# One transformer-like layer on one core: modulation sums by TensorE, smaller first pieces of tile 0, and a second copy in the Fourier stage

## The chip, the core and the metric

The kernel runs on one core of a Trainium2 chip. The core has five engines with an instruction queue each: TensorE (PE, matrix products, with its weight loads shown apart as PEld), VectorE (DVE), ScalarE (ACT), GpSimd (POOL) and SyncE (SP, which here only issues transfers). Each engine works through its instructions in the order in which they stand in its program and waits at an instruction until its semaphores allow it. Transfers are issued by SP, ACT and POOL into DMA queues and moved by 16 DMA engines. Products go into eight PSUM banks of 128 x 512 floats; everything else lies in SBUF, with 128 partitions.

The metric is the device time of one execution in microseconds. An L with a number is a line of the kernel before, unless the changed kernel is meant and said.

## The reference, cut to what matters

One layer is computed for two groups of tokens that share parameters: 256 context tokens and 2,048 latent tokens, each with 1,024 channels, which makes 18 tiles of 128 rows. All of it is fp32.

```python
def adaln(cvec, w_mod, b_mod):                 # modulation: two vectors (c and c_ctx)
    m = jax.nn.silu(cvec) @ w_mod + b_mod      # 1024 -> 6 x 1024
    return jnp.split(m[:, None, :], 6, axis=-1)

sh1, sc1, g1, sh2, sc2, g2 = adaln(...)
h = rms_norm(x, norm1_g) * (1 + sc1) + sh1
q, k, v, f = split(h @ w_in)                   # 4 x 512 columns
attn = softmax(q0 k0) v - lam * softmax(q1 k1) v          # 4 heads, latent keys + 512 cached keys
spec = fft2(f, axes=(positions, 128 channels), norm='ortho').real   # 4 channel groups
four = spec @ w_four                           # per channel group
x = x + g1 * (concat(rms_norm(attn), four) @ w_out)
x = x + g2 * relu(rms_norm(x)*(1+sc2)+sh2 @ w1)**2 @ w2
```

Only the first two parts of `m` (shift `sh1`, scale `sc1`) are needed before the first tile's projection. The 2-D transform is done as real matrix products: over the positions with cosine and sine matrices, then over the channels.

## The kernel before, in words

**Order of the work.** The kernel is one long function, `body`, that runs through its stages in turn: modulation and the first tile; projection of the 18 tiles; the Fourier stage; attention of the four heads; output projection and MLP. In most places the instructions stand on each engine in the order in which the code issues them (`manual_schedule`); tiles in the middle of the projection and later stages are ordered by a scheduler. Each matrix product that needs fp32 accuracy is made of three with a high and a low part of each operand (L94, L95, L96 in `mm3`): high x high, high activation x low weight, low activation x high weight.

**Modulation (L464 to L538).** Eight blocks `wm` of 128 rows of `w_mod` are loaded, 2,048 columns each (the 1,024 of the shift and the 1,024 of the scale). Columns 0 to 1,279 are multiplied by PE (`pr`, L484, two rows for two conditioning vectors). Columns 1,280 to 2,047 are summed up by VectorE: `acc[s]` for each of the two vectors `s`, 128 x 768, to which each block adds its rows times a number per partition (L486 to L490). In between stand the normalization of the first tile's rows and PE's transposes of them (L495, into the two banks `pt0`). At the end the sums must become columns. For the PE part, ScalarE copies `pr` to `mr` and PE transposes it in pieces of 128 into `pm` (L535, ten small transposes). For the VectorE part, what is left is the sum over the 128 partitions: VectorE transposes blocks of 32 and adds within them (`TRANSPOSE_TENSOR_REDUCE`, L528, once for each `s`) and PE adds the four blocks with a matrix of shifted ones, `quad0`, which GpSimd has made at the start (L474, `quads`): four products into `pq` (L537). VectorE then adds the bias into `modc` and makes `scale1 = (1 + scale) * gain` (`mk_scale`).

**Tile 0.** The weights `w_in` come in sixteen half blocks of 1,024 columns (`w_half`, L504; k is the block of 128 rows, h the half), of which six buffers exist. ScalarE rounds them to the high part (`w_high`, L513), VectorE subtracts for the low part (`w_rest`, L516), and each second `w_rest` asks for the half block six further on, by a DMA on SP's queue. Tile 0's transposed rows are scaled and shifted out of PSUM into `h0` (`h_first`, in two pieces of four column blocks) and split into a high and a low part, `hh` and `hl` (L554, L555). The projection `pj` of tile 0 follows block by block, so that its products start as soon as the first half of `hh` is there, and each block's four column groups `g` wait for that block's weights.

**Fourier (L643 to L985).** Its pools are opened in the order `f_t`, `f_y`, `f_l` on the left side of SBUF. A pool lies behind the one opened ahead of it, and pools with `reuse_waits="tile"` take over memory of closed pools: a new tile waits for whatever still uses the bytes that it takes.

```python
ft = c2.enter_context(tc.tile_pool(name="f_t", bufs=2, reuse_waits="tile"))
yp = c2.enter_context(tc.tile_pool(name="f_y", bufs=1, reuse_waits="tile"))
```

For each channel group g of four, `f_y` holds `ys{g}`, 128 x 2,048 floats, into which all results of that group are put. The work runs over levels named `p` (context tokens), `o`, `e`, `f` and `l` by size. In a level PE first makes two products over the positions (`pab`, evacuated by ScalarE into `abe`, `abf`, `abl` and so on, L792 and L810), and then `yT` (L749) makes two over the channels, `py` (L753) and `pz` (L755), that rotate through three PSUM banks. ScalarE copies `py` to an SBUF buffer `yu` (L759). VectorE subtracts and adds the pair into two halves of `ys` (L767, L768), reading `yu` from SBUF and `pz` from PSUM. `yu` has two buffers in `f_t` for widths up to 256, and four in `f_l` for the widest level, where `pz` is copied also (`yv`) and the additions are put off. When the last level has filled `ys{g}`, GpSimd's queue issues its store of 1 MiB into the scratch `four` in HBM (L829); the stores of g = 0, 1, 2, 3 follow one another.

**Attention.** Its pools follow when those of the Fourier stage are closed (L992 to L1000): `a_t`, then `a_p` with five buffers `P0` of 10,240 bytes per partition, on the same side of SBUF, and PSUM as 5 + 2 + 1 banks. For a block of 128 queries PE makes scores `Ss` of 512 keys at a time (`fill`, L1080), VectorE takes their maximum over the row (`rowmax`, L1085, and `comb`, L1088), ScalarE takes the exponential from the PSUM bank into `P0` or `P1` (`exp`, L1104), which empties the bank, GpSimd scales and combines the two halves (L1119, L1120), and PE transposes the result (L1135) for the product with the values. The first two groups use all eight banks for scores (`Group.bank`, L1059), so PE may be eight banks ahead of ScalarE.

## Time and profile before

| | |
|---|---|
| median of 3 runs | 2862.53 us (2861.9 to 2864.64) |
| the profiled execution | 2863.18 us, its span 2861.4 us |
| mean granted TensorE clock | 0.999 |
| modulation and tile 0 | from the start to about 60 us |
| Fourier stage | ends at about 520 us |
| attention's first exponential | at 522.70 us |

The profile is of one execution; its times count from the span's start. How rows read: a line of engines says busy time, share of the span and number of instructions. A row of the waits names an engine, the instruction that waited, the engine and instruction that released it, the total in us, how often, and the longest. A row of the order in time has the start and the duration in us, the engine, line, operation, out<-in, their shapes, how many, and in square brackets how long the engine had been idle ahead of it and what released it. A row of the windows has the stretch, its length, and then the busy time (with the count of instructions) of PE, PEld, DVE, ACT and POOL, the granted clock, the share of the DMA engines and GB/s. A row of the groups has busy time, the mean ns of one, and the idle time just ahead with its releaser.

### The profile page before, as it was taken

The numbers are of one execution on the slowest core, as the hardware profiler recorded it, in microseconds if no ns is written. First come the engines' busy times: TensorE is split into PE (matmuls) and PEld (weight loads), VectorE is DVE, ScalarE is ACT, GpSimd is POOL, SyncE is SP. The second block draws the span as 40 slices with busy tenths as digits, with TensorE's granted clock in tenths as the row PEclk, the third lists the DMA queues.
The fourth block names the chain that finished last, engine by engine and source line by source line (L and its number), as shares of the span: only waits on it lengthen the run. The fifth ranks groups of instructions, "written<-read, shape, count | busy, mean of one in ns | idle before, by whom it ended". The sixth has DMA issues, their size and how long they took to land.

```text
span 2861.4 us, 43224 instructions
## 1 busy us (share of the span) xinstructions
PE 2831.7 (99%) x15109; PEld 2455.9 (86%) x15109; DVE 2018.0 (71%) x3393; ACT 1548.2 (54%) x3505; POOL 1073.3 (38%) x890
## 2 busy tenths in 40 slices
PE   8999999999999999999999999999999999999999
PEld 5888888688888888888889999999998888888887
DVE  7767886898988989864477777778775354345554
ACT  4333323798989989853356565556555332333221
POOL 1211223798999989942223333333332000000000
PEclk9999999999999999999999999999999999999999
DMA  7776777421211212036767676667747464445663
GB/s 284 219 207 198 230 213 237 172 106 38 73 71 53 106 38 99 23 124 201 242 221 232 223 246 228 221 219 238 234 167 255 147 202 135 138 144 185 206 206 111
DMA packets 392780, 492.94 MB, mean 172 GB/s; under 512 B 26467, under 2 KB 306384, under 8 KB 389490
## 3 DMA queue, kind: packets, MB, share of 16 engines
q1 hardware_dynamic: 387136, 479.73, 50.9%
q0 software_dynamic: 1872, 7.28, 0.8%
q10 hardware_dynamic: 3554, 3.17, 0.4%
q8 instruction: 119, 1.95, 0.3%
q14 instruction: 99, 0.81, 0.1%
HBM read 312.58 MB, written 179.59 MB: 172 GB/s over the span
## 4 chain that ended last, share of the span: by engine, by line
PE 54%; DVE 1%; DMA 0%; ACT 0%; issue 0%; SPq 0%; POOL 0%; DVEq 0%; POOLq 0%
PE ps L94 8%; PE ps L95 8%; PE ps L96 8%; PE pB L1749 2%; PE pB L1747 2%; PE pB L1748 2%; PE pA L1748 2%; PE pC L1748 2%; PE pA L1749 2%; PE pC L1747 2%; PE pA L1747 2%; PE pC L1749 2%; PE po L94 2%; PE po L96 2%; PE po L95 2%; PE pD L1749 1%
## 5 line engine op out<-in xcount | busy, mean ns | idle before, releaser
L1085 DVE TENSOR_REDUCE mxs<-Ss 128x1 f32<-128x512 f32 x636 | 405.4, 686 | 65.5 <-PE Ss L1080 55.1
L1420 DVE TENSOR_TENSOR sl<-sr,sh 128x768 fp32r<-128x768 f32 x168 | 161.8, 964 | 331.5 <-ACT sh L1419 331.1
L1120 POOL TENSOR_TENSOR P0s<-P0s,P1s 128x1024 f32<-128x1024 f32 (+2 forms) x128 | 378.6, 2958 | 10.7
L1419 ACT CAST sh<-sr 128x768 fp32r<-128x768 f32 x168 | 140.6, 838 | 418.3 <-PE ps L95 418.3
L1789 POOL TENSOR_TENSOR gs<-g,g 128x384 f32<-128x384 f32 x48 | 69.7, 1452 | 468.5 <-ACT g L1759 418.9
L1104 ACT ACTIVATE P1s<-Ss,mxs 128x512 f32<-128x512 f32 x318 | 215.4, 694 | 36.3 <-DVE mxs L1088 35.3
L94 PE MATMUL pj<-wh,hh 128*128 128x512 f32 x576 | 228.8, 397 | 2.0 <-DVE hh L555 2.0
L94 PE MATMUL ps<-thT,sh 128*128 128x512 f32 x585 | 227.6, 389 | 0.0
L95 PE MATMUL ps<-tlT,sh 128*128 128x512 f32 x585 | 227.6, 389 | 0.0
L96 PE MATMUL ps<-thT,sl 128*128 128x512 f32 x585 | 227.6, 389 | 0.0
L95 PE MATMUL pj<-wl,hh 128*128 128x512 f32 x576 | 227.1, 394 | 0.5 <-DVE wl L516 0.5
L96 PE MATMUL pj<-wh,hl 128*128 128x512 f32 x576 | 225.6, 392 | 0.0
L1104 ACT ACTIVATE P0s<-Ss,mxs 128x512 f32<-128x512 f32 x318 | 214.3, 691 | 5.6 <-DVE mxs L1088 5.0
L1135 PE MATMUL pts<-ident,P0s 128*128 128x128 f32 x1280 | 191.7, 273 | 4.5 <-DVE als L1147 1.8
L1080 PE MATMUL Ss<-KS0s,Qs 128*128 128x512 f32 x636 | 190.1, 419 | 0.4 <-ACT P1s L1104 0.4
L1080 PE MATMUL Ss<-KS1s,Qs 128*128 128x512 f32 x636 | 188.7, 420 | 1.5 <-ACT P0s L1104 1.4
L1758 ACT ACTIVATE g<-uz 128x384 f32<-128x384 f32 x144 | 75.7, 526 | 200.2 <-DVE uz L1781 174.1
L1135 PEld LDWEIGHTS pts<-ident,P0s 128*128 128x128 f32 x1280 | 151.3, 140 | 35.9 <-issue 4.8
L1119 POOL TENSOR_SCALAR P1s<-P1s,tots 128x1024 f32<-128x1024 f32 (+2 forms) x128 | 171.9, 1343 | 5.8
L1147 DVE TENSOR_TENSOR als<-pts,ahs 128x512 fp32r<-128x512 f32 x256 | 165.9, 681 | 6.9 <-ACT ahs L1142 6.7
L94 PE MATMUL ps<-ophT,sh 128*128 128x512 f32 x423 | 164.7, 389 | 1.1 <-DVE uz L1781 1.1
L96 PE MATMUL ps<-ophT,sl 128*128 128x512 f32 x423 | 164.6, 389 | 0.0
(536 smaller groups left out, 8073.9 us busy)
## 6 DMA issues: line engine op xcount, KB each, us to landing
sr<-sd SPq DMA_DIRECT2D x84, 768.0 KB, 4.5
a<-in_w SPq DMA_DIRECT2D x184, 256.0 KB, 4.2
sd<-gs SPq DMA_DIRECT2D x192, 192.0 KB, 1.9
sd<-g SPq DMA_DIRECT2D x144, 192.0 KB, 2.1
wm<-in_w_mod SPq DMA_DIRECT2D x32, 512.0 KB, 5.2
Qs<-qd SPq DMA_DIRECT2D x32, 512.0 KB, 4.0
b<-in_w SPq DMA_DIRECT2D x64, 256.0 KB, 5.8
b<-tsum SPq DMA_DIRECT2D x64, 256.0 KB, 4.7
```

The source lines that it names most:

```text
L94: nc.tensor.matmul(ps, lh, rh, start=first, stop=False)
L95: nc.tensor.matmul(ps, lh, rl, start=False, stop=False)
L96: nc.tensor.matmul(ps, ll, rh, start=False, stop=last)
L1080: nc.tensor.matmul(S[:, :w], self.Q[:, x, m, j * P:j * P + P], self.hd.KS[m][:, b * 512:b * 512 + w], start=(x == 0), stop=(x == 1))
L1085: nc.vector.tensor_reduce(self.mx[j][:, m, b:b + 1], self.S[j, m, b], axis=AX.X, op=ALU.max)
L1104: nc.scalar.activation(dst, S, AF.Exp, bias=self.mx[j][:, m, 6:7], accum_out=self.sm[j][:, m, b:b + 1])
L1119: nc.gpsimd.tensor_scalar(p, p, tot[:, 3:4], 0.0, op0=ALU.mult, op1=ALU.add)
L1120: nc.gpsimd.tensor_add(d, d, p)
L1135: nc.tensor.transpose(pt[:, c:c + P], self.p0[j][:, (kb + t) * P:(kb + t + 1) * P], ident)
L1747: nc.tensor.matmul(ps, wh[:, c], hh[:, k, :], start=first and k == 0, stop=False, skip_group_check=True)
L1748: nc.tensor.matmul(ps, wh[:, c], hl[:, k, :], start=False, stop=False, skip_group_check=True)
L1749: nc.tensor.matmul(ps, wl[:, c], hh[:, k, :], start=False, stop=k == 3, skip_group_check=True)
```

## The change

It has three parts.

*Modulation.* `quad0`, VectorE's two transposing reductions and the four products with them are gone. PE makes the sums over the partitions by twelve products, six for each `s`: 128 columns of `acc[s]` as the stationary matrix and the column `ones` as the moving one, straight into `pq` (L540 of the changed kernel). `s` runs as (1, 0) here and in the sums over the blocks. The transposes of the tile's column blocks 6 and 7 move from ahead of the last `wm` block to the small transposes.

*Tile 0.* `h_first(b)`, which did four column blocks, becomes `h_pieces(ks)`, called with (0, 1), (2, 3) and (4 to 7); the scale is made for the first two blocks alone and then for the others (`scale_part`). The weights' steps `w_high` and `w_rest` of column groups 0 and 1 are issued ahead of the scaling, with them the request for half block 6; `w_high` of groups 2 and 3 stands between the pieces.

*Fourier.* `yu` has four buffers in `f_t` too. For the widths 256 and 128 ScalarE copies `pz` also, to the upper half of `yu`, and VectorE's subtraction and addition read SBUF alone. For 129 columns (levels `p` and `l`) `pz` is read from PSUM as before.

```diff
                     setup_cond(p1, pps, rw)
-                    z = quads(t2, "quad0")
+                    for n in range(2):
+                        t2(f"place{n}")
...
-                        for s in range(2):
+                        for s in (1, 0):
                             wk, sc = wm[k][:, 1280:2048], cols[:, 8 * s + k:8 * s + k + 1]
...
-                        if 3 <= k < 7:
+                        if 3 <= k < 6:
...
-                    sums = t2("sums0")[:, 0:48].rearrange("p (s c) -> p s c", s=2)
-                    for s in range(2):
-                        nc.vector.tensor_reduce(sums[:, s, :], acc[s].rearrange("p (c i) -> p c i", i=32), axis=AX.X, op=ALU.add,
-                                                apply_transpose=True)
+                    w_high(0, 0)
+                    w_rest(0, 0)
                     for gi in range(3):
...
+                        if gi == 2:
+                            for x in (6, 7):
+                                nc.tensor.transpose(at0(x), X[0][:, x * P:(x + 1) * P], ident)
+                            X.pop(0)
                         for j in range(w // P):
                             nc.tensor.transpose(pm[:, gi * 4 + j, :], r[0:2, j * P:(j + 1) * P], ident[0:2, 0:2])
-                    for q in range(4):
-                        nc.tensor.matmul(pq, z[:, 96 - 32 * q:224 - 32 * q], sums[:, :, q::4], start=(q == 0), stop=(q == 3))
-                    for g in range(4):
-                        w_high(0, g)
-                    w_rest(0, 0)
...
-                    mk_scale(scale1, 8, 80)
+                    for s in (1, 0):
+                        for j in range(6):
+                            nc.tensor.matmul(pq[:, s, j:j + 1], acc[s][:, j * P:j * P + P], ones, start=True, stop=True)
+                    w_high(0, 1)
+                    w_rest(0, 1)
...
-                    def h_first(b):
-                        for k in range(4 * b, 4 * b + 4):
...
+                    def h_pieces(ks):
+                        for k in ks:
...
+                    nc.vector.tensor_add(modc[:, 0:10, :], pm, cols[:, 32:42].unsqueeze(2).to_broadcast([P, 10, 2]))
+                    scale_part(slice(0, 2))
+                    h_pieces((0, 1))
+                    nc.vector.tensor_add(modc[:, 10:16, :], pq.rearrange("p s j -> p j s"), cols[:, 42:48].unsqueeze(2).to_broadcast([P, 6, 2]))
+                    scale_part(slice(2, KD))
+                    for g in (2, 3):
+                        w_high(0, g)
+                    h_pieces((2, 3))
...
-                            if k or g:
+                            if k or g > 1:
                                 w_rest(k, g)
...
-                            h_first(1)
+                            h_pieces((4, 5, 6, 7))
...
-                u, v = (yl if late else ft).tile([P, 512], F32, tag="yu", name="yu", bufs=4 if late else 2)[:, :w], pz[:, :w]
+                yu = (yl if late else ft).tile([P, 512], F32, tag="yu", name="yu", bufs=4)
+                u, v = yu[:, :w], pz[:, :w]
                 nc.scalar.copy(u, py[:, :w])
...
+                elif w != HW:
+                    v = yu[:, 256:256 + w]
+                    nc.scalar.copy(v, pz[:, :w])
```

Three places in the order of the instructions show it. A row has the line, the operation, out<-in with the tiles' numbers, the shape, and the semaphores that it waits for; `x3` stands for three more of the kind.

PE at the end of the modulation, before: small transposes of `mr` into `pm10`, the four products with `quad0`, and the first three projections of tile 0.

```order
L535 MATMUL pm10_402<-ident_175,mr1_413 128x2 [waits Activation_49]
L535 MATMUL pm10_402<-ident_175,mr1_413 128x2 x3
L535 MATMUL pm10_402<-ident_175,mr2_419 128x2 [waits Activation_49]
L535 MATMUL pm10_402<-ident_175,mr2_419 128x2
L537 MATMUL pm6_403<-sums0_404,quad0_249 128x12 [waits DVE_49,Pool_49]
L537 MATMUL pm6_403<-sums0_404,quad0_249 128x12 x3
L94 MATMUL pj0_0_456<-wh0_0_337,hh0_436 128x512 [waits DVE_49]
L95 MATMUL pj0_0_456<-wl0_0_345,hh0_436 128x512
L96 MATMUL pj0_0_456<-wh0_0_337,hl0_437 128x512 [waits DVE_49]
```

The same place in the changed kernel; `macc_l` and `macc_h` are the two `acc[s]`.

```order
L537 MATMUL pm10_397<-ident_175,mr1_407 128x2 [waits Activation_49]
L537 MATMUL pm10_397<-ident_175,mr1_407 128x2 x3
L534 MATMUL pta0_1_255<-ident_175,x0_226 128x128 x2
L537 MATMUL pm10_397<-ident_175,mr2_413 128x2 [waits Activation_49]
L537 MATMUL pm10_397<-ident_175,mr2_413 128x2
L540 MATMUL pm6_398<-ones_182,macc_l_257 128x1 [waits DVE_49]
L540 MATMUL pm6_398<-ones_182,macc_l_257 128x1 x5
L540 MATMUL pm6_398<-ones_182,macc_h_256 128x1 [waits DVE_49]
L540 MATMUL pm6_398<-ones_182,macc_h_256 128x1 x5
L94 MATMUL pj0_0_465<-wh0_0_332,hh0_435 128x512 [waits DVE_49]
L95 MATMUL pj0_0_465<-wl0_0_340,hh0_435 128x512
```

The transposes of `x0` now stand among the small ones, and twelve products with `ones`, which wait for VectorE's last sums, take the place of the four that waited for VectorE's reductions.

ScalarE in the Fourier stage, before, from the last `yu` of level `e` to level `f`.

```order
L759 COPY yu_5073<-py_5069 128x256 [waits DVE_49,PE_49]
L792 COPY abf0_0_5083<-pabf0_0_5081 128x128 [waits PE_49]
L792 COPY abf0_1_5087<-pabf0_1_5085 128x128 [waits PE_49,Activation_49]
L759 COPY yu_5093<-py_5089 128x256 [waits PE_49]
L792 COPY abf1_0_5099<-pabf1_0_5097 128x128 [waits PE_49]
L792 COPY abf1_1_5103<-pabf1_1_5101 128x128 [waits PE_49,Activation_49]
L759 COPY yu_5109<-py_5105 128x128 [waits PE_49]
```

The same place in the changed kernel.

```order
L773 COPY yu_5081<-py_5077 128x256 [waits DVE_49,PE_49]
L779 COPY yu_5081<-pz_5079 128x256 [waits PE_49]
L809 COPY abf0_0_5092<-pabf0_0_5090 128x128 [waits PE_49]
L809 COPY abf0_1_5096<-pabf0_1_5094 128x128 [waits PE_49,Activation_49]
L773 COPY yu_5102<-py_5098 128x256 [waits DVE_49,PE_49]
L779 COPY yu_5102<-pz_5100 128x256 [waits PE_49]
L809 COPY abf1_0_5109<-pabf1_0_5107 128x128 [waits PE_49]
L809 COPY abf1_1_5113<-pabf1_1_5111 128x128 [waits PE_49,Activation_49]
L773 COPY yu_5119<-py_5115 128x128 [waits DVE_49,PE_49]
```

Each copy of `py` into `yu` has a copy of `pz` into the same buffer behind it.

ScalarE at the passage from the Fourier stage to the attention, before: the last copies of the Fourier stage and the first exponential.

```order
L810 COPY abl3_0_5204<-pabl3_0_5201 128x130 [waits PE_49]
L810 COPY abl3_1_5209<-pabl3_1_5206 128x130 [waits PE_49,Activation_49]
L759 COPY yu_5215<-py_5211 128x129 [waits PE_49]
L759 COPY yu_5224<-py_5220 128x129 [waits PE_49]
L1104 ACTIVATE P0s0_0_0_5294,sms0_0_0_5271<-Ss0_0_0_0_0_5273,mxs0_0_0_5270 128x512 [waits DVE_49,Pool_49]
```

The same place in the changed kernel.

```order
L827 COPY abl3_0_5218<-pabl3_0_5215 128x130 [waits PE_49]
L827 COPY abl3_1_5223<-pabl3_1_5220 128x130 [waits PE_49,Activation_49]
L773 COPY yu_5229<-py_5225 128x129 [waits PE_49]
L773 COPY yu_5238<-py_5234 128x129 [waits PE_49]
L1121 ACTIVATE P0s0_0_0_5308,sms0_0_0_5285<-Ss0_0_0_0_0_5287,mxs0_0_0_5284 128x512 [waits DMASW0_49,DVE_49,Pool_49]
```

The first exponential, which waited for VectorE and for GpSimd, now waits for a DMA of GpSimd's queue as well (`DMASW0`). By the counts behind these names in the two programs it is the queue's last transfer in the Fourier stage, the store of `four` from `ys3`.

20 lines of the change are left out of this document (11 added, 9 removed).

## The prediction

> **What bounds the kernel now.** I read the page first, then TensorE's list of waits for the two stretches that the change touches, then the order in time at each wait found there.
>
> ```profile
> span 2861.4 us, 43224 instructions
> PE 2831.7 (99%) x15109; PEld 2455.9 (86%) x15109; DVE 2018.0 (71%) x3393; ACT 1548.2 (54%) x3505; POOL 1073.3 (38%) x890
> PE pj L94 <- DVE hh L555: 2.0, 1, 2.0
> PE ptckT L358 <- DMA ck<-in_cache_k: 1.2, 2, 0.9
> PE pj L95 <- DVE wl L516: 0.5, 1, 0.5
> PE pz L755 <- DVE ys L768: 1.4, 1, 1.4
> 560.00:600.00 40.00, 40.00 (x264) 34.21 (x264) 35.34 (x72) 36.85 (x103) 37.91 (x28) 1.00 0.25 96
> ```
>
> TensorE (PE) is busy for 99% of the span, and the three lines after it are all that it waited for by name from 30 to 492 us: 3.7 us. So an edit can win only what stands in such lines, and whatever newly stops PE is lost whole. The Fourier stage adds one wait of 1.4 us (fourth line of waits). In the attention (last row: 40 us in which PE is busy for 40.00) there is no idle time that could give a loss back. All terms below are against this execution, 2863.18 us with a span of 2861.4; it lies 0.65 above the median, 2862.53. What a measurement here can tell from no change is about 0.2%, 5.7 us.
>
> **Tile 0 and the modulation.**
>
> ```profile
> 28.53 0.93 DVE L528 TRANSPOSE_TENSOR_REDUCE sums<-macc_l 128x24 f32<-128x768 f32 x1
> 28.59 0.85 PE L535 MATMUL pm<-ident,mr 2*128 2x2 f32 x10
> 29.61 1.03 PE L537 MATMUL pm<-sums,quad 128*128 128x12 f32 x8 [0.17 <-DVE sums L528]
> 32.62 0.79 PE L94 MATMUL pj<-wh,hh 128*128 128x512 f32 x1 [1.98 <-DVE hh L555]
> 31.00:32.00 1.00, 0.00 (x0) 0.00 (x0) 0.93 (x4) 0.88 (x4) 0.00 (x0) 0.50 1.00 410
> 37.00:38.00 1.00, 1.00 (x4) 0.81 (x3) 1.00 (x3) 1.00 (x3) 0.00 (x0) 0.65 0.95 332
> 47.26 2.39 ACT L513 CAST wh<-win 128x512 fp32r<-128x512 f32 x4 [0.65 <-DMA win<-in_w_in]
> 53.67 2.50 DVE L516 TENSOR_TENSOR wl<-win,wh 128x512 fp32r<-128x512 f32 x4 [0.28 <-ACT wh L513]
> 55.25 0.50 PE L94 MATMUL pj<-wh,hh 128*128 128x512 f32 x1
> 56.23 0.50 PE L95 MATMUL pj<-wl,hh 128*128 128x512 f32 x1 [0.47 <-DVE wl L516]
> ```
>
> Removed: VectorE's (DVE's) two reductions (one shown, 0.93; the pair takes 1.9) and four fp32 products that run as 8 passes in 1.03 us, 0.129 each. Added: twelve products with the column of ones, 24 passes; at 0.129 that is 3.1 us. They stand behind the ten small transposes, which end at 29.44, so PE is free at about 32.5. Tile 0's first pieces don't hold it up: VectorE needs the sum into `modc`, two steps of the scale, one scaled piece, a copy and a subtraction of half the size, some 1.8 us from about 29.9. So the first projection starts at 32.5 against 32.62 now: nothing won, unless the passes run at half clock (the row 31 to 32 has a granted clock of 0.50), which would make it up to 33.4.
>
> That start doesn't set the end of the stage. The last rows do: PE lost 0.75 us between its products at 55.25 and 56.23 (0.98 from start to start, against 0.23 in steady state), because the last weight's low part came from a chain that begins with a load (ScalarE waited 0.65 us for it at 47.26) and then runs without a gap over ScalarE (ACT) and VectorE. The change requests one weight load some 4 us sooner, since the low part of column group 1 no longer stands behind the scaling, and every later step of VectorE about 0.6 us later. With the early load out of the queue's way I take the 0.75 us as won. Bounds: 2.3 us won if the products keep the clock up (the 11 steps from 32.62 to 37.48 take 4.86 us and would take 2.5 at full clock), 1.0 lost if VectorE's 0.6 and a late start both come through. I take 0.75, nearest to the stall in the rows. The quad matrix on GpSimd (four small steps in the first 2.6 us) costs nothing now and wins nothing.
>
> **Fourier.**
>
> ```profile
> 509.56 0.39 PE L753 MATMUL py<-abf,cw 128*128 128x128 f32 x2
> 511.39 0.49 PE L755 MATMUL pz<-abf,cw 128*128 128x128 f32 x2 [1.44 <-DVE ys L768]
> 510.71 0.62 DVE L768 TENSOR_TENSOR ys<-yu,pz 128x256 f32<-128x256 f32 x1
> 503.09 0.84 DVE L777 TENSOR_TENSOR ys<-yu 128x256 f32<-128x256 f32 x1
> L792 ACT COPY abe<-pabe 128x256 f32<-128x256 f32 x6 | 2.2, 372 | 4.2 <-PE pabe L800 4.2
> ```
>
> PE's one stall here is 1.44 us: the product `pz` needs a bank that VectorE empties at 511.33, behind other work. With ScalarE copying `pz` the bank is free after one copy, so the stall goes: 1.44 won. Added: four copies of 256 and four of 128 columns, priced like its `abe` and `abf` copies, 0.37 and 0.27, 2.6 us in all; they lie in its idle time (4.2 us before six copies in the last row). If that cover were gone, PE would wait for each `ab` copy. VectorE's 16 operations now read both operands from SBUF; between 0.62 (now) and 0.84 (a 128x256 operation on SBUF beside busy GpSimd) the eight wide ones would cost it at most 1.8 us, and that makes the stores below later, not PE.
>
> **Where the new buffers lie.** `yu` has four buffers where it had two: 4,096 bytes per partition more in pool `f_t`, and `f_y` and `f_l` are laid out behind it. By the addresses in the two built programs `ys3` moves from bytes 75,776-83,968 to 79,872-88,064, and the attention's first `P0` block begins at 84,608 in both. Before, the last store (`four` from `ys3`) and the first exponential shared nothing; now the block overlaps the store's source by 3,456 bytes, and the exponential waits for it (third order excerpt above).
>
> ```profile
> 516.49 0.55 POOL L829 DMA_DIRECT2D four<-ys  x1 [5.55 <-DVE ys L768]
> 520.05 0.53 POOL L829 DMA_DIRECT2D four<-ys  x1 [0.35 <-issue]
> DMA to landing us min/median/max: 9.0/11.5/14.7
> q0 software_dynamic: 159, 1.13, 89.2%
> DMA packets 319, 1.28 MB, mean 427 GB/s; under 512 B 42, under 2 KB 172, under 8 KB 181
> 522.70 0.69 ACT L1104 ACTIVATE P0s<-Ss,mxs 128x512 f32<-128x512 f32 x1 [4.04 <-DVE mxs L1088]
> 529.35 0.74 ACT L1104 ACTIVATE P0s<-Ss,mxs 128x512 f32<-128x512 f32 x1
> 523.53 1.40 PE L1080 MATMUL Ss<-KS1s,Qs 128*128 128x512 f32 x4 [1.12 <-ACT P0s L1104]
> ```
>
> The four stores of 1 MiB each queue behind one another, so I give the last, issued at 520.05, the longest of the landing times, 14.7: it lands at 534.75. The first exponential starts at 522.70 now. In the changed kernel the stage is 0.75 + 1.44 us earlier, so the store lands at 534.75 - 2.19 = 532.56, and the exponential starts there: 9.86 us later than now. Queued behind it on ScalarE are all other exponentials, which run without a gap (ten in 6.65 us by the rows at 522.70 and 529.35). PE fills eight banks of scores and then waits (at 523.53 it waited for the first exponential already); VectorE's maxima wait for PE. Nothing else can go ahead, so the 9.86 is the whole kernel's. Both gains are swallowed: they only bring the store forward.
>
> Ends: 12.05, if the landing doesn't move at all; 5.9, if the stores have the engines to themselves (rival two). I take 9.86, since it keeps the latency of the row.
>
> A wait of 11 us on PE (from about 521.3) has its own price. The rows at 31 and 37 show it: PE idle for 1.98 us, clock 0.50, back in the slice 37 to 38, 5.1 us after PE had started again. At half clock a bank of scores takes two products of 0.427 (the spacing from 32.62 on), 0.85, against ScalarE's pace of 0.66: 0.19 short for six or seven banks, 1.2 at most and 0 if the eight full banks carry ScalarE over it. I take 0.6. [...]
>
> Sum: 2863.18 + 9.86 + 0.6 = 2873.6 against the profiled execution, 2873.0 against the median.
>
> **Rivals.** *Two: the stores drain faster.* All queues together moved 0.427 MB per us at best (row above, 524 to 527, of which the stores' queue had 1.13 of 1.28 MB). Alone, 4.19 MB take 9.8 us; their first bytes moved at about 521, so 518.8 less the gains: landing at 528.6, 5.9 us lost, 2868.4. Against it: loads of the attention share the engines until 535. [...] *Four, not slower:* the wait isn't met, because the store lands before the exponential is ready at 520.5; then the two gains stand, 2862.53 - 2.19 = 2860.3. It decides as soon as the landing takes no more than 2.6 us from an issue at 517.9; the row's minimum of 9.0 speaks against it. *Five, worse:* the landing stays at 534.75 or moves later, because VectorE's slower additions delay the stores or tile 0 loses, and the clock costs 1.2: 2862.53 + 12.05 + 1.2 = 2875.8, with 1.0 more from tile 0 some 2877.
>
> **How the numbers follow.** The forecast has 0.65, rival two 0.08, three 0.03, four 0.04, five 0.20. The range goes from rival two's 2868.4 to five's 2877. Slower by over 0.2% means above 2868.3: forecast, five and about half of two, 0.89. Within it: the rest of two, three and nearly all of four, 0.10. Faster by more would need 5.7 us won where PE's waits hold 3.6 together: 0.01.
>
> **What would show it.** After: an idle time of about 11 us on ScalarE before the first exponential, released by the DMA of `four<-ys`, PE idle as long, and a granted clock below 1 behind it; no wait of `pz` on VectorE; no TRANSPOSE_TENSOR_REDUCE before 30 us, PE's first projection between 32.3 and 33.4, and little left of the 0.47 at the last weight. The forecast is wrong if the last store lands within 6 us of its issue, or if PE has full banks to work on while ScalarE waits.

## The result: slower by 16.5 us, more than forecast

The changed kernel takes 2879.16 us (median of 4 runs, 2876.88 to 2879.88) against 2862.62 for the kernel before: ratio 1.0055, 95% interval 1.0042 to 1.0067. The interval does not take in a ratio of 1, so the change is slower. The forecast was 2873.0 us, with a range from 2868.4 to 2877.0. The direction and the place of the main loss were right; the size was not.

First the page of the changed kernel (its profiled execution took 2879.88 us) and TensorE's waits up to 560 us. From here on an L is a line of the kernel that the rows are of.

```profile
span 2878.1 us, 43246 instructions
PE 2837.7 (99%) x15125; PEld 2463.5 (86%) x15125; DVE 2019.0 (70%) x3395; ACT 1549.3 (54%) x3513; POOL 1072.0 (37%) x886
PE Ss L1097 <- ACT P0s L1121: 13.1, 1, 13.1
PE pabl L825 <- DVE s256s L854: 1.2, 1, 1.2
PE pj L94 <- ACT wh L513: 0.7, 1, 0.7
PE pj L95 <- DVE wl L516: 0.5, 1, 0.5
```

The 13.1 us are new, so are the waits of 1.2 and 0.7, and the 0.5 at the last weight's low part has stayed. The waits at `pz` and for the first `hh` are gone. Next ScalarE around the first exponential, the four stores on GpSimd's queue (first and last), and the longest time from a store's issue to its landing:

```profile
521.28 0.27 ACT L773 COPY yu<-py 128x129 f32<-128x129 f32 x1 [0.18 <-PE py L766]
537.57 0.69 ACT L1121 ACTIVATE P0s<-Ss,mxs 128x512 f32<-128x512 f32 x1 [16.02 <-DMA four<-ys]
519.38 0.55 POOL L846 DMA_DIRECT2D four<-ys  x1 [5.41 <-DVE ys L785]
522.93 0.53 POOL L846 DMA_DIRECT2D four<-ys  x1 [0.34 <-issue]
DMA to landing us min/median/max: 2.9/6.7/14.5
```

The exponential waits for the store of `four` from `ys3`, as forecast: issued at 522.93, landed 14.5 us later at 537.43, exponential at 537.57 (522.70 before). But the store was issued 2.88 us later than before (520.05), and the forecast had it 2.19 sooner.

The table shows where the lag comes from: by how much the same instruction of VectorE, ScalarE or GpSimd starts later in the changed kernel's profile than in the one before (median over a stretch, or the instruction named).

```
place (time in the kernel before)                      lag, us
120 to 180, projection, behind tile 0                    3.65
260 to 280                                               3.88
320 to 500, behind a wait for cached keys                2.76
last store issued (520.05)                               2.88
first exponential (522.70)                              14.87
530 to 540                                              15.44
580 to 860                                              16.43
end                                                     16.68
```

So 3.65 us were lost in the first stage and 0.2 more by 270, of which 1.1 came back near 285; the Fourier stage added 0.1, the wait 12.0, the clock behind it 1.6 (0.57 up to 540 and 1.0 by 580), and the rest of the kernel 0.2. These are two single executions, and the first rows are less certain than they look: tile 0's last low part ends at 56.17 us in the profile before and at 57.61 in that of `bufs_only` below, whose first stage has the same instructions. The windows show the clock (last three columns: granted clock, DMA share, GB/s; the clock before was 1.00 in all of them):

```profile
525.00:530.00 5.00, 0.28 (x2) 0.00 (x0) 2.25 (x5) 0.00 (x0) 0.00 (x0) 0.90 1.00 412
530.00:535.00 5.00, 0.00 (x0) 0.00 (x0) 0.00 (x0) 0.00 (x0) 0.00 (x0) 0.50 1.02 423
535.00:540.00 5.00, 1.60 (x4) 1.27 (x5) 0.34 (x1) 2.43 (x7) 0.00 (x0) 0.50 0.85 335
540.00:545.00 5.00, 5.00 (x17) 3.27 (x15) 4.58 (x10) 4.48 (x14) 0.00 (x0) 0.74 0.00 0
560.00:565.00 5.00, 4.33 (x15) 3.12 (x14) 3.18 (x5) 3.54 (x10) 4.83 (x4) 0.69 0.01 3
```

From 530 to 535 no engine works at all, and the DMA engines are full (share 1.02): the whole core waits for the stores, with loads moving beside them.

### The profile page after: what moved, and what is told of

It reads as the page before. It is cut to its first block, busy times and chain, and to the rows that moved or that the text cites. A ratio compares the mean times of both kernels' runs of the same rounds, so it can differ in the third digit from the quotient of the medians.

```text
span 2878.1 us, 43246 instructions
## 1 busy us (share of the span) xinstructions
PE 2837.7 (99%) x15125; PEld 2463.5 (86%) x15125; DVE 2019.0 (70%) x3395; ACT 1549.3 (54%) x3513; POOL 1072.0 (37%) x886
## 4 chain that ended last, share of the span: by engine, by line
PE 92%; DVE 2%; DMA 2%; POOL 1%; ACT 1%; issue 1%; SPq 0%; ACTq 0%; DVEq 0%; POOLq 0%
PE Ss L1097 10%; PE ps L94 8%; PE ps L95 8%; PE ps L96 8%; PE pts L1152 5%; PE po L96 4%; PE po L94 4%; PE po L95 4%; PE pj L95 4%; PE pj L96 4%; PE pj L94 4%; PE pB L1765 2%; PE pB L1764 2%; PE pB L1766 2%; PE pC L1764 2%; PE pA L1765 2%
## 5 line engine op out<-in xcount | busy, mean ns | idle before, releaser
L1097 PE MATMUL Ss<-KS1s,Qs 128*128 128x512 f32 x636 | 190.2, 424 | 13.3 <-ACT P0s L1121 13.1
```

Source lines behind the costliest of these rows:

```text
L1097: nc.tensor.matmul(S[:, :w], self.Q[:, x, m, j * P:j * P + P], self.hd.KS[m][:, b * 512:b * 512 + w], start=(x == 0), stop=(x == 1))
```

## Experiments

The theory after this reading had three parts: the placement of the buffers costs about 13 us with its clock; the modulation and tile 0 cost some 2.8; the copies of the Fourier stage win nothing because VectorE became slower. Each part was tried alone. Each group of runs was made on another chip, and the kernel before was timed again beside it: 2863.09 us beside `bufs_only`, `rev`, `right` and `tile0`, 2863.58 beside `ones_only`, `pieces_only`, `ones_first` and `right_psum`, and 2862.79 beside the others.

### Where the buffers lie

**Four buffers and nothing else** (`bufs_only`).

```diff
-... tag="yu", name="yu", bufs=4 if late else 2)[:, :w], pz[:, :w]
+... tag="yu", name="yu", bufs=4)[:, :w], pz[:, :w]
```

> The kernel before, with four buffers of yu in f_t where it had two, and nothing else: no copy more, the modulation and tile 0 as before. My theory: placement alone brings the wait. The last store is issued at 520.05 as before and lands 14.5 us later, at 534.6; the exponential moves from 522.70 to there, +11.9, and half clock adds 1.0 to 1.8: 2875.5 to 2876.5 us. Rival (the copies make the wait, by delaying the stores or loading ScalarE): within 2 us of 2862.6.

Measured: 2876.73 us (2875.99 to 2878.05), ratio 1.0048, interval 1.0033 to 1.0063. ScalarE's and TensorE's waits:

```profile
ACT P0s L1104 <- DMA four<-ys: 16.0, 1, 16.0
PE Ss L1080 <- ACT P0s L1104: 13.1, 1, 13.1
```

Two buffers more, without one instruction more, cost 13.6 us of the 16.5. That settles the main cause: the copies do not make this wait.

**Which store is waited for** (`rev`).

```diff
-ys = [yp.tile([P, NS], ..., name=f"ys{g}") for g in range(4)]
+ys = [yp.tile([P, NS], ..., name=f"ys{g}") for g in (3, 2, 1, 0)][::-1]
```

> The changed kernel, but the four ys lie in reverse order of addresses, so that the first P0 block overlaps ys0, whose store is the first of the four to be issued (519.38 in the profile of the changed kernel) and not the last (522.93). My theory: the exponential waits for that one landing. If the four stores land one behind the other, the first lands some 9 us after its issue (the shortest landing time of the four before), at 528.4, and the exponential starts there and not at 537.6; 2879.2 - 9 - some half clock = about 2870 us. If the stores share the engines evenly, all four land near 537 and nothing changes: about 2879. Rival (the wait isn't for ys's bytes): 2879 too, but with the wait still put down to the last store.

Measured: 2869.31 us (2868.17 to 2871.92), ratio 1.0022, interval 1.0013 to 1.0031.

```profile
517.54 0.56 POOL L846 DMA_DIRECT2D four<-ys  x1 [6.03 <-DVE ys L785]
527.06 0.69 ACT L1121 ACTIVATE P0s<-Ss,mxs 128x512 f32<-128x512 f32 x1 [4.71 <-DMA four<-ys]
```

With `ys0` under the first `P0` block the exponential starts 9.5 us after the first store's issue and not 14.6 after the last one's. The four stores land one behind the other, at 526.96, 530.10, 532.90 and 535.84, and the wait goes to whichever `ys` shares bytes with the block.

**The overlap taken away** (`right`): two of the four buffers lie in pool `f_w`, on the other side.

```diff
-yu = (yl if late else ft).tile([P, 512], F32, tag="yu", name="yu", bufs=4)
+yu = (yl.tile(..., bufs=4) if late else (ft, fw)[len(YU) % 2].tile(..., tag="yu", bufs=2))
...                                   # the list YU counts the tiles, so that the two pools take turns
```

> The changed kernel, but the two additional buffers of yu lie in the pool f_w on the other side of SBUF, so that ys3 keeps its old bytes and the first exponential waits for no store. My theory: the overlap of ys3 and the first P0 block costs 12.0 us of waiting and about 1.8 of half clock behind it, and the rest of the loss (2.8 us) was there before the stores; so 2862.6 + 2.8 = 2865.4 us, between 2864.5 and 2866.5, and the first exponential at about 525.6. Rival: the copies or the store traffic cost the time by themselves (DMA engines, ScalarE), and the wait is only where it shows; then it stays above 2874.

Measured: 2869.67 us (2867.72 to 2871.43), ratio 1.0021, interval 1.0012 to 1.0031. The wait for the store is gone, but the first exponential stands at 529.01, not at 525.6, and the total is 4.3 us above the theory's and 4.3 below the rival's. The windows and TensorE's waits of the profiled execution, the slowest of the ten (2871.43 us), show why:

```profile
510.00:515.00 5.00, 3.64 (x31) 3.31 (x29) 5.00 (x8) 3.04 (x14) 2.92 (x4) 1.00 0.02 3
515.00:520.00 5.00, 5.00 (x30) 5.00 (x28) 3.03 (x12) 2.08 (x8) 0.43 (x1) 0.58 0.89 324
520.00:525.00 5.00, 5.00 (x23) 4.90 (x23) 1.61 (x6) 1.61 (x6) 0.97 (x3) 0.50 0.92 324
PE pabl L827 <- DVE s256s L856: 1.2, 1, 1.2
```

TensorE waited 1.2 us for VectorE near 513, and then the last level of the Fourier stage ran at half clock, 515.8 to 526.0. The lag grew there from 1.7 to 6.3 us. The ten runs have a mean granted clock of 0.996 to 0.998, against 0.998 to 0.999 for the kernel before, so half clock came in most of them. In the profile of the changed kernel the same wait left the clock at 1.00 until 528.96, so it does not come each time, and there the wait for the store would have covered it anyway.

### Modulation and tile 0

**Both parts without the Fourier change** (`tile0`): the changed kernel with the lines of `yT` as before.

> The changed kernel with the Fourier stage as before: modulation sums by TensorE and tile 0 in smaller pieces alone. My theory: the first stage is 3.65 us later at its end and 0.9 of it is taken up by a load's wait near 285 us, so +2.8: 2865.4 us, with no wait at the first exponential. What was forecast (0.75 won here): 2861.9. Rival (the lag of the first stage is swallowed by waits further on): within 1 us of 2862.6.

Measured: 2865.06 us (2862.72 to 2866.81), ratio 1.0007, interval 0.9998 to 1.0017. By the medians 2.0 us are lost, near the theory and not the 0.75 won that was forecast, but the interval takes in no change. With the placement's 13.6 this makes 15.6 of the 16.5, by medians alone.

The stretch in the changed kernel's trace: PE's sums (24 passes) and first projection, VectorE's wait for them, then the weights' low parts behind it, and the waits at the last weight.

```profile
30.23 2.40 PE L540 MATMUL pm<-ones,macc_l 128*128 128x1 f32 x12
32.49 2.70 PE L540 MATMUL pm<-ones,macc_h 128*128 128x1 f32 x12
35.05 0.77 PE L94 MATMUL pj<-wh,hh 128*128 128x512 f32 x1
35.22 0.17 DVE L567 TENSOR_TENSOR modc<-pm,cols 128x12 f32<-128x12 f32 x1 [2.24 <-PE pm L540]
37.57 1.28 DVE L516 TENSOR_TENSOR wl<-win,wh 128x512 fp32r<-128x512 f32 x2
38.92 0.33 SPq L507 DMA_DIRECT2D win<-in_w_in  x1
58.91 0.50 PE L94 MATMUL pj<-wh,hh 128*128 128x512 f32 x1 [0.68 <-ACT wh L513]
59.88 0.50 PE L95 MATMUL pj<-wl,hh 128*128 128x512 f32 x1 [0.47 <-DVE wl L516]
```

The sums take 4.8 us (0.2 a pass at half clock). VectorE stands at `modc` for 2.24 us, and the low parts of column groups 2 and 3, with the request for the next half block at 38.92, stand in its queue behind `modc` and the second piece.

How much of that is the change, and how much this one execution? The same first stage was profiled in several kernels:

```
first stage    kernel        first projection   last low part, end
as before      before            32.62              56.17
               bufs_only         32.79              57.61
as changed     changed           35.05              59.83
               tile0             34.15              58.76
               right             34.08              59.42
               rev               32.91              57.67
               right_psum        33.27              59.48
               right_dve         34.17              59.06
```

The means are 59.04 and 56.89, 2.1 us apart, like the medians of the times; the changed kernel's profile is the latest of its six. In `bufs_only` ScalarE waited 2.31 and 1.24 us for two weight loads where it waited 1.72 and 0.65 before, which is most of the 1.4 us between these two. In `rev` the 24 passes ran at full clock (2.70 us, rows in the last section), and its projection starts within what was forecast; its last low part is still 1.5 later than before's. Which part of the change makes the 2 us? Four runs were made on it.

**Products with ones alone** (`ones_only`) and **pieces and weight steps alone** (`pieces_only`), each on the kernel before.

```diff
 ones_only
-... (the two reductions of VectorE)
-for q in range(4):
-    nc.tensor.matmul(pq, z[:, ...], sums[:, :, q::4], ...)
+for s in range(2):
+    for j in range(6):
+        nc.tensor.matmul(pq[:, s, j:j + 1], acc[s][:, j * P:j * P + P], ones, start=True, stop=True)
 pieces_only: h_pieces, scale_part, the weights' order, the order (1, 0) of s and the
 late transposes of column blocks 6 and 7, all of the changed kernel,
 with the two reductions and the four products with quad0 kept
```

> The kernel before, with the sums over partitions made by the twelve products with the column of ones in the place of the reductions and the four products; the pieces of tile 0 and the order of the weights' steps as before, the Fourier stage as before. My theory: the loss of the first stage comes from these products (0.20 us a pass, 24 passes, 4.8 us against 1.2 + 0.7 of waiting before), and from VectorE and ScalarE, which hold the scaling behind their sum and the weights' steps behind the scaling; so the first projection starts near 36 us (32.62 before), the stage ends 3 to 4 us later, and after the 1.1 that a wait near 285 us takes up the total is 2864.8 to 2866. Rival (the smaller pieces and the moved weight steps make the loss): first projection near 33, total within 0.7 us of 2863.1.

> The smaller pieces and the weights' steps of the changed kernel, with the sums over partitions by VectorE's reductions and the four products as before; Fourier stage as before. My theory: the sum is there by 31 us, nothing is held up, and the stage ends where it did or up to 0.8 us sooner: 2862.0 to 2863.3. Rival (pieces and moved steps make the loss): near 2865.

Measured: 2864.20 us (2863.20 to 2865.87), ratio 1.0002, interval 0.9993 to 1.0011, and 2865.78 us (2864.25 to 2867.32), ratio 1.0006, interval 0.9997 to 1.0015. The medians (+0.6 and +2.2) lie nearer to the rival than to the theory that the products alone do it, while the first projection of `ones_only`, at 35.85, is where the theory had it; the intervals tell neither time from nothing. The traces, one execution each, have both stages later than before's, in the table below.

**The products ahead of the small transposes** (`ones_first`, on `tile0`).

```diff
+for s in (1, 0):
+    for j in range(6):
+        nc.tensor.matmul(pq[:, s, j:j + 1], acc[s][:, ...], ones, start=True, stop=True)
 w_high(0, 0)
 w_rest(0, 0)
 for gi in range(3):
     ... (copies mr, small transposes)
-for s in (1, 0): ... (the same products)
```

> The changed modulation and tile 0 (Fourier stage as before), with the twelve products with ones issued straight behind the last product of pr, ahead of the small transposes, so that they run while PE would wait for ScalarE's copy. If a pass takes 0.10 us there (the clock is at full until about 31 us), the sum is there at 30.8, the transposes follow by 31.7 and the first projection starts near 33: 2862.5 to 2863.8. If a pass takes 0.20 us at any clock, the sum is there at 33.1, the first projection starts near 35.5, and it is as slow as the changed first stage alone, 2865.

Measured: 2866.44 us (2865.37 to 2870.26), ratio 1.0011, interval 1.0001 to 1.0021: not better. The first twelve passes took 0.113 us each, near the first case of what was expected, but the projection starts at 35.14, as in the second. The passes now end near 31.2 and the small transposes behind them at 33.2 (30.3 in the changed kernel), and the first scaled piece, which needs these, waits for them instead.

**The weights' steps ahead of the wait** (`weights_ahead`, on `tile0`).

```diff
 h_pieces((0, 1))
+for g in (2, 3):
+    w_high(0, g)
+    w_rest(0, g)
 nc.vector.tensor_add(modc[:, 10:16, :], ...)
 scale_part(slice(2, KD))
-for g in (2, 3):
-    w_high(0, g)
 h_pieces((2, 3))
...
-if k or g > 1:
+if k:
     w_rest(k, g)
```

> The changed modulation and tile 0 (Fourier stage as before), with the weights' steps of column groups 2 and 3 of the first block (ScalarE's and VectorE's) issued behind the first scaled piece and ahead of the wait for the sum of the products with ones. The second half block that is asked for (the eighth in all) leaves as soon as VectorE has done the low part of group 3. In all five kernels so far its request stands 0.06 us behind that step, and the last low part of tile 0 ends 20.7 to 21.9 us behind the request. My theory now: this chain (low part, request, load, high part, low part) sets the end of tile 0, not the start of the first projection. Then VectorE does the steps while it would wait for PE (1.4 us here), the request goes out near 34.3 (38.03 in this first stage as changed), later requests gain what VectorE no longer idles, some 1 to 1.4 us, the last low part ends near 57.5 (58.76), and the total is 2863.6 to 2864.5 against 2865.1. Rival (PE's passes at half clock and its late start set the end): last low part and total unchanged, 2865.

Measured: 2864.04 us (2862.73 to 2865.29), ratio 1.0003, interval 0.9994 to 1.0012. The time lies where the theory had it, 1.25 above the kernel before beside it where `tile0` was 1.97 above its own, though both intervals take in no change. The steps do not all follow the theory: the request goes out at 34.18, as expected, but the last low part ends at 58.25 and not at 57.5. The fixed distance of 21 us from that request was no law; later requests wait for other steps of VectorE. The table has VectorE's idle time (worked out from its busy time in the window 28 to 40 us, of 12 us) beside the end of tile 0's last low part:

```
kernel          first        VectorE idle    low part g=3,      last low
                projection   28 to 40        first block, end   part, end
before            32.62         0.72             35.16            56.17
changed           35.05         5.01             38.86            59.83
tile0             34.15         4.12             37.96            58.76
ones_only         35.85         5.24             38.39            59.61
pieces_only       32.53         1.42             36.48            58.20
ones_first        35.14         5.25             39.09            61.02
weights_ahead     33.06         3.41             34.15            58.25
```

Where VectorE idles longer for the sums, the stage mostly ends later: 4.3 us more idle and 3.7 later in the changed kernel, 2.7 and 2.1 in `weights_ahead`. It is no rule, since `bufs_only` idles 0.72 like before and ends 1.4 later for its loads. `pieces_only` has little idle and is still 2.0 late, with 1.3 of it before the first block's last low part; its smaller pieces put waits between ScalarE and VectorE and more small steps into the queue. How much each step of that costs, and how much is the loads of that execution, was not separated.

### The Fourier stage

VectorE's additions of 128 x 256 before (first two rows, L767 and L768) and in the changed kernel (busy us and mean ns of one), rows of both engines of the changed kernel in order of time, and PE's wait:

```profile
L767 DVE TENSOR_TENSOR ys<-yu,pz 128x256 f32<-128x256 f32 x4 | 2.5, 624 | 0.4 <-PE pz L755 0.4
L768 DVE TENSOR_TENSOR ys<-yu,pz 128x256 f32<-128x256 f32 x4 | 2.6, 640 | 0.0
L784 DVE TENSOR_TENSOR ys<-yu 128x256 f32<-128x256 f32 x4 | 4.5, 1136 | 0.0
L785 DVE TENSOR_TENSOR ys<-yu 128x256 f32<-128x256 f32 x4 | 4.5, 1124 | 0.0
508.77 1.40 POOL L790 TENSOR_TENSOR yu<-yu,yv 128x512 f32<-128x512 f32 x1
509.00 1.65 DVE L785 TENSOR_TENSOR ys<-yu 128x256 f32<-128x256 f32 x1
512.97 1.00 POOL L795 TENSOR_TENSOR ys<-yu 128x256 f32<-128x256 f32 x1
515.49 0.61 DVE L784 TENSOR_TENSOR ys<-yu 128x256 f32<-128x256 f32 x1
515.02 0.44 PE L825 MATMUL pabl<-c,s256s 128*128 128x65 f32 x2 [1.20 <-DVE s256s L854]
```

They take 1.13 us in the mean, up to 1.69, against 0.63 before; the last pair, behind GpSimd's last addition, takes 0.61 and 0.63 again. Each of the six slow ones ends 0.48 to 0.51 us behind the end of a GpSimd instruction (here 508.77 + 1.40 and 509.00 + 1.65), as if it had waited for that end. `s256s`, which stands behind these six in VectorE's queue, is late, and PE waits 1.20 us for it, nearly what the bank at `pz` no longer costs. Two runs on the layout of `right` test the cause.

**Copies made but not read** (`right_psum`).

```diff
-v = yu[:, 256:256 + w]
-nc.scalar.copy(v, pz[:, :w])
+nc.scalar.copy(yu[:, 256:256 + w], pz[:, :w])
```

> The changed kernel with two yu buffers on the other side (no wait at the first exponential), and ScalarE's copies of pz made but not read: VectorE takes pz from PSUM as before. With the copies read, VectorE's 128x256 operations took 1.1 to 1.7 us while GpSimd was at work, and PE then waited 1.2 us for s256s. My theory: it is the second SBUF operand beside GpSimd that makes them slow. Then they take 0.62 to 0.65 here, the wait for s256s is gone, the 1.4 us at pz is back, and the time falls from 2869.7 to that of the changed first stage alone, 2865. Rival (the eight copies on ScalarE delay VectorE, or the buffers on the other side cost the time): VectorE still slow or waiting, 2868 or more.

Measured: 2865.92 us (2863.62 to 2866.76), ratio 1.0007, interval 0.9998 to 1.0016.

```profile
L785 DVE TENSOR_TENSOR ys<-yu,pz 128x256 f32<-128x256 f32 x4 | 2.5, 623 | 0.8 <-ACT yu L780 0.8
L786 DVE TENSOR_TENSOR ys<-yu,pz 128x256 f32<-128x256 f32 x4 | 2.6, 639 | 0.0
```

With the same copies on ScalarE, VectorE is fast, the wait for `s256s` and the half clock of the Fourier stage are gone, and 1.3 us at `pz` are back. The operand that VectorE reads is all that differs from `right`, so the 3.8 us between the medians are its price (4.2 when each is taken against the kernel before beside it).

**GpSimd's additions on VectorE** (`right_dve`).

```diff
-V = nc.gpsimd if g == 3 else nc.vector
+V = nc.vector
...
-nc.gpsimd.tensor_add(dst[:, 0:256], de, do)
-nc.gpsimd.tensor_sub(mirror_dst[:, 511:255:-1], de, do)
+nc.vector.tensor_add(dst[:, 0:256], de, do)
+nc.vector.tensor_sub(mirror_dst[:, 511:255:-1], de, do)
```

> The changed kernel with two yu buffers on the other side (no wait at the first exponential, 2869.7), and GpSimd's additions of the Fourier stage on VectorE. My theory: VectorE's 128x256 operations with both operands in SBUF are slow (1.13 us in the mean) only beside a busy GpSimd. Then all eight take 0.60 to 0.65 here. VectorE has some 20 more operations of 128x256 or 128x512, about 13 us more work between 480 and 515, so the time of the whole says little: 2866 to 2880. Rival (SBUF against PSUM alone makes the difference): they still take 1.1 us.

Measured: 2867.09 us (2865.08 to 2868.06), ratio 1.0014, interval 1.0005 to 1.0023.

```profile
L786 DVE TENSOR_TENSOR ys<-yu 128x256 f32<-128x256 f32 x4 | 2.5, 628 | 0.0
L787 DVE TENSOR_TENSOR ys<-yu 128x256 f32<-128x256 f32 x4 | 2.5, 636 | 0.0
PE Ss L1099 <- DMA Qs<-qd: 3.7, 1, 3.7
```

Both operands in SBUF and GpSimd silent: 0.63 us. So it takes both, the second SBUF operand and a busy GpSimd. In this profile the lag falls from 1.9 us ahead of the Fourier stage to 0.0 at its end, more than `pz`'s 1.44; but then PE waits 3.7 us for `Q` of the next group. That its load is late because it shares the DMA engines with the four stores was not tried and is a guess (the longest landing of a `Q` in this run is 8.5 us, the median 3.9).

Side by side, for VectorE's additions of 128 x 256: with GpSimd at work 1.13 us in the mean with both inputs in SBUF (changed kernel) and 0.63 with one of them in PSUM (`right_psum`), and 0.63 with both in SBUF and GpSimd silent (`right_dve`). What makes it so was not shown, and whether GpSimd is held up in turn these rows don't tell.

### Looking for a version that keeps the gain

**One copy only** (`best`), on the kernel before: the last product of level `e`, whose bank PE waited for, and the second tile's scaling behind the second block's weight steps.

```diff
+elif w == 256 and g == 3:
+    v = yu[:, 256:256 + w]
+    nc.scalar.copy(v, pz[:, :w])
...
-if k == 0:
-    norm_scale(X[1])
 if k == 1:
+    norm_scale(X[1])
     h_first(1)
```

> The kernel before with two small edits. In the Fourier stage ScalarE copies pz for one product alone, the last of level e (256 columns, channel group 3), whose bank held PE up for 1.44 us; two buffers as before, no other copy, so nothing moves in SBUF and VectorE's other additions read PSUM as before. In tile 0 the scaling of the second tile's rows (VectorE, 0.75 us) stands behind the second block's weight steps and not ahead of them. My theory: the wait at pz goes (1.4 us) and no wait for s256s takes its place, since VectorE is not slowed; the weights' chain gains up to 0.75, so PE's 0.75 at the last weight goes too. 2863.3 - 2.1 = 2861.2, between 2860.7 and 2862.0. Rivals: the stall moves to the next product (2863), or the late rows hold up PE's transposes (2863.5).

Measured: 2864.64 us (2861.82 to 2868.45), ratio 1.0009, interval 1.0000 to 1.0017. The stall moved by one product (first row): ScalarE's next copy into `yu` waited 1.89 us for VectorE to empty a buffer and held up `abf`. **With four buffers on two sides** (`best4`; the edit of `right` added):

> The kernel before with the copy of pz for the last product of level e alone and the rows' scaling of the second tile moved behind the second block's weight steps, as in the run ahead, but with four yu buffers, two of them in the pool f_w on the other side of SBUF. With two buffers PE's wait did not go away: ScalarE's copy into yu waited for VectorE to empty it, and the copies of abf queued behind it (PE waited 1.9 us for abf, and the clock fell to half for 3.4 us). My theory: with four buffers ScalarE does not wait, the 1.4 us at pz goes, no half clock follows, and 0.4 to 0.6 us of tile 0 are kept: 2862.8 - 1.4 - 0.6 = 2860.8 us. Rivals: the stores and the loads of the attention's Q, V fill the DMA engines until 535 us whatever the Fourier stage wins, so that PE waits for Q and nothing is won, 2862.5 to 2863.5; or VectorE is still late for s256s and the half clock comes back, 2865.

Measured: 2866.41 us (2862.64 to 2871.54), ratio 1.0012, interval 1.0003 to 1.0021. It moved again, to the next bank that VectorE empties (second row), and 1.86 us of waiting were followed by half clock from 511.3 to 525.0.

```profile
PE py L752 <- ACT abf L795: 1.9, 1, 1.9
PE py L752 <- DVE ys L773: 1.9, 1, 1.9
515.00:520.00 5.00, 5.00 (x25) 5.00 (x25) 1.12 (x5) 1.61 (x6) 0.55 (x1) 0.50 0.96 376
```

The runs of `best4` with a mean granted clock of 0.999 took 2862.64 to 2863.80 us, those at 0.996 and 0.997 took 2866.41 to 2871.54; for `best` it is 2861.82 to 2864.02 at 0.999 and 2866.98 to 2868.45 at 0.997. So the half clock makes most of the loss, and without it nothing is won either. Tile 0's last low part ended at 55.74 and 55.65 in these two, 0.4 to 0.5 sooner than before, which is less than single executions differ by.

So the bank at `pz` was where PE happened to meet VectorE's lateness (VectorE does `s256s` and `s256d` there, 2.2 us), not its cause. No version was found that beats the kernel before.

## Why the prediction was wrong, point by point

Against its profiled execution the prediction had 2873.6 and the changed kernel's has 2879.88, a miss of 6.3 us.

- **Where the new buffers lie**: right in place, mechanism and latency. The landing took 14.5 us (forecast 14.7), and the exponential moved by 11.99 us beyond the stage's own lag (12.05 by the same working). That the copies are not needed for it was shown by `bufs_only`.
- **The step that failed: the 2.19 us by which the stage was to be earlier.** In the profile the stage was 2.88 later, which makes 5.1 of the miss. The medians say the same: `bufs_only`, the placement alone, costs 13.6 us and the whole change 16.5, so the rest of the change cost 2.9 where it was to bring the store 2.19 forward. Its two terms:
  - *Tile 0, "I take the 0.75 us as won".* It lost 3.65 in the profile and some 2 us by the medians and over the six profiles of this first stage. A pass was taken at 0.129 us, 3.1 in all, and PE's start at 32.5. In the changed kernel's profile the passes ran at half clock at 0.2, 4.8 in all, and PE started at 35.05, beyond the 33.4 that was given as the worst; in `rev` they ran at full clock and PE started at 32.91, so this part hangs on where the half clock falls. But `rev` lost 1.5 in the stage all the same. "Every later step of VectorE about 0.6 us later" left out that VectorE waits for the sums with the weights' low parts behind it: the first block's last one came 3.7 us later in the changed kernel. The early request of one half block won nothing that shows; the one behind it left at 38.92.
  - *Fourier, "1.44 won".* The wait at `pz` did go, but VectorE's eight additions cost 4.0 us more (eight times 1.13 less 0.63), where 1.8 was given as the most, from a 128x256 operation of 0.84 beside GpSimd. That price was of another operation: alone it takes 0.42 (`right_dve`, L796), so it had already doubled, and these take 0.63 alone. And "that makes the stores below later, not PE" was wrong: PE waited 1.20 us for `s256s`, in VectorE's queue behind them. Net 0.1 lost.
- **The clock: 0.6 forecast, 1.57 measured.** Half clock lasted from 528.96 to 542.61, behind the restart nearly as long as forecast (4.2 us, forecast 5.1), and cost 0.57 there. A second stretch, 559.67 to 563.09, was not forecast and goes with the other 1.0. `bufs_only` has none there and its lag grows by 0.1, and `pieces_only` and `weights_ahead`, without the store's wait, have such stretches near 545, so this part is not of the change alone.
- **Rivals.** Two and three (stores faster, three still more so) and four (no wait) fell with the 14.5 us. Five named just these causes, slower additions and a loss in tile 0, and came nearest with 2877, 2.2 too little. In the chances, "PE's waits hold 3.6 together" is a slip, since the rows that the change could touch (2.0, 0.5 and 1.4) make 3.9; nothing hangs on it.
- **What was to show it**: the idle ScalarE, the idle PE and the half clock were there (16.02 with the 4 that it idles anyway, 13.1, 0.50), `pz` no longer waits. The first projection at 32.3 to 33.4 and the vanished wait at the last weight were not.

## What to carry to other kernels

A buffer more is also an address: look which later tile begins where the pools now end, and what transfer still reads there; this was 13.6 of 16.5 us and needed no instruction. When an operand is moved from PSUM to SBUF, price the instruction beside what GpSimd does at that time (1.13 us against 0.63 here), and follow the slow engine's queue to the next instruction that PE waits for. A wait that is put into an engine's queue also holds up what stands behind it there (2.24 us at `modc` in VectorE's), so look which steps depend on nothing and could go ahead of it; `weights_ahead` did that and stood 0.7 us nearer to its kernel before than `tile0` did, which the intervals don't confirm. And before a difference of one or two microseconds between two profiles is explained, look at the same instructions in a third: unchanged ones differed by 1.4 us here.

## What the runs showed of the hardware

The products with one moving column ran at 0.113 us a pass at full clock (24 passes in 2.70 us, by the starts in `rev`, the first three rows) and at 0.21 at half (12 passes from 32.49 to 35.05 in the changed kernel's rows above). Having PE busy with them did not keep the clock up. In `rev` PE was busy without a gap from 30.21 on, and the clock fell at 33.78, 0.9 us after their end; in the changed kernel it fell at 30.61, behind a wait of 0.58 us, and stayed at half while they ran and PE was busy throughout (last two rows, columns as in the windows above):

```profile
30.21 1.50 PE L540 MATMUL pm<-ones,macc_l 128*128 128x1 f32 x12
31.57 1.48 PE L540 MATMUL pm<-ones,macc_h 128*128 128x1 f32 x12
32.91 0.49 PE L94 MATMUL pj<-wh,hh 128*128 128x512 f32 x1
30.00:32.00 2.00, 2.00 (x13) 1.97 (x13) 1.33 (x5) 0.75 (x3) 0.00 (x0) 0.65 1.03 420
32.00:34.00 2.00, 2.00 (x11) 2.00 (x11) 0.91 (x3) 0.77 (x2) 0.00 (x0) 0.50 1.05 426
```

The trace's record of the granted clock up to 700 us, in us from the span's start:

```
half clock in       tile 0            from 510 us on
before              30.88 to 37.71    none
changed             30.61 to 40.85    528.96 to 542.61, 559.67 to 563.09
bufs_only           31.30 to 38.12    529.64 to 543.30
rev                 33.78 to 40.60    515.06 to 521.88, 528.71 to 532.12
right               31.10 to 37.93    515.80 to 526.04, 549.93 to 553.34
pieces_only         33.84 to 40.67    545.84 to 549.25, 552.66 to 556.08
weights_ahead       32.72 to 36.13    544.72 to 548.13
best4               33.46 to 36.87    511.32 to 524.97, 548.87 to 552.28
```

In these eight traces each stretch lasted 1, 2, 3 or 4 times 3.41 us (3.41 to 13.65), within one trace they lie on one grid (in the changed kernel 528.96 is 143 times 3.413 us behind 40.85, a third of its first stretch of 10.24), and the first one begins at another place in each execution, 30.61 to 33.84. It fits that the same stall sometimes costs a stretch of half clock and sometimes none: the eleven runs of `best4` lie 9 us apart and go with their mean clocks, the four of `bufs_only` 2. Which stalls bring a stretch of half clock was not settled: 1.44 us at `pz` did not in the kernel before nor 1.20 in the changed kernel's profile, 1.18 to 1.88 did in `right`, `rev`, `best` and `best4`.
